# A tuned two-layer expert network on one core: the tasks that choose experts and build gates are cut in two, and one norm's rows go to another PSUM bank

## The chip, the core and the metric

The kernel runs on one core of a Trainium2 chip. The core has a matrix engine (PE, with its weight loads shown apart as PEld), a vector engine (DVE), a scalar engine (ACT), a general engine (POOL) and a queue that issues DMAs (SP). Each engine takes its instructions in the order in which the program lists them, and the engines wait for one another through semaphores. SBUF is the working memory; PSUM holds the results of matmuls in eight banks of 512 f32 per partition. The metric is the device time of one execution in microseconds (us); lower is better.

## What is computed

256 tokens of width 1024 pass through two layers and then a third block with two gated feed-forwards (`ffn1`, `ffn2`) around a token mixer. In each of the two layers a mixer is followed by this expert step (`peer`):

```python
q = (t @ w_q).reshape(n_tok, 8, 2, 128)
sc = jnp.einsum('thpd,hpnd->thpn', q, sub_keys)
s1, i1 = lax.top_k(sc[:, :, 0], 16)
s2, i2 = lax.top_k(sc[:, :, 1], 16)
cand = (s1[..., :, None] + s2[..., None, :]).reshape(n_tok, 8, 256)
top_s, pos = lax.top_k(cand, 16)
eidx = jnp.take_along_axis(cidx, pos, axis=-1)
gate = jax.nn.softmax(top_s, axis=-1)
hid = jax.nn.gelu(jnp.einsum('td,thkd->thk', tc, u[ec]), approximate=False)
out = jnp.einsum('thk,thkd->td', gc * hid, v[ec])
```

So each token has, for each of 8 heads, two lists of 128 scores; the 16 best of each list give 256 sums, and the 16 best sums name 16 of 16384 experts. The kernel multiplies all 16384 rows of `u` and `v` and lets the gates be zero for those not chosen. Everything is f32; each f32 product is made of three matmuls over a high and a low part.

## The kernel before

**Weights.** Every matrix comes from HBM as a sequence of 128x1024 f32 tiles, about 800 in all. For each tile SP issues a DMA into `wraw` (3 buffers), ACT rounds it to the high part `whi` (L178), DVE subtracts to get the low part `wlo` (L179), both with 3 buffers, and PE uses the pair in 24 matmuls (L350 to L352: `hi` by `hi`, `hi` by `lo`, `lo` by `hi`, eight times). The first instruction that needs `wlo` is the third of the 24, on L352. `W.get()` for tile k first issues the rounding and the split of tile k+2. So the split of a tile is issued up to two tiles ahead of its use and can't run further ahead, since its buffers are those of the tile that PE has just left. The next DMA into a `wraw` buffer waits until both ACT and DVE have read it.

**Side work.** Between weight tiles other work is put into the engines' streams by a small list of tasks (`Tasks`). Each task has a cost, a number written into the code; `bg.tick(budget)` is called once for each weight tile, adds its budget to a credit, and runs tasks from the front of the list as long as the credit is above zero. The cost only decides at which tile a task's instructions stand; how long they take is another matter. While `u` is multiplied the budget is 1.35 for a tile (`TK_U`), later the mean that empties the list (`bg.spread`).

**The choice of experts.** `peer` is called twice (layer 0 and layer 1). For each of two tiles of 128 tokens (`tt`) and four pairs of heads (`g`), `chosen(tt, g)` queues a group of tasks: two `keys16` (each the 16 best of two lists of 128), `make_cand` (the sums), `cand16` (the 16 best of two lists of 256), `gate_a`, `gate_b`, `gate_c` (softmax of the best, and the experts' numbers by one-hot products), and for `tt` 0 the writing of numbers and a scatter by POOL. That is eight groups a layer, spread over the 16 tiles of `w_q` and about the first 70 of the 128 tiles of `u`. The scores come from PE and ACT, the softmax's `exp` is ACT's; the rest of a group is DVE's. The 16 best are found by `top16`, five instructions for a list: the best 8 (MAX8), their places (FIND_INDEX8), the list without them (MATCH_REPLACE8), again the best 8 and their places; where places or values are looked up a short MATCH_VALUE_LOAD runs first. `top16` gets two lists at a time and alternates between them, step by step.

**The gates.** `gates(half, ...)` builds the dense gates of 8 tokens a step for token tile 1: `make` (DVE, and POOL for the second half), `mult` (16 short matmuls), `fold` (DVE multiplies the result from PSUM into the hidden values). One task runs `mult` of the step before, `make`, and `fold` of two steps before. Half 0 lies in the second part of `u`, half 1 in the first half of `v`.

**PSUM.** Two pools share the eight banks: `mm` (4, for the main products) and `acc` (4, for the sums of `v` and for side work). In `ffn1` the norm object `TwoNorms` makes two sets of per-token factors. `n.bcast()` spreads the first over all partitions (short matmuls into a bank, copied out by ACT on L452) and `n.settle()`, called from `after()`, spreads the second in the same way and queues the scaling of `h`. Both take the bank from `n.newps`, here `mmtile`.

Of the kernel before, what the change touches and what calls it, by code (L numbers as in the profile page):

```python
# [277 lines left out]
def _program(tc, nc, glob, wpool, mmp, accp, drp, ins, out, scat, stop):  # L278
# [16 lines left out]
    h = glob.tile([128, 8, TALL], F32, name="h")  # L295
# [16 lines left out]
    bg = Tasks()  # L312
# [23 lines left out]
    gcol, at = {}, 0  # L336
# [470 lines left out]
    def peer(l, n, close_parts, open_parts):  # L807
# [11 lines left out]
        gt0 = sp.tile([128, 128], F32, name="gt0")  # L819
# [10 lines left out]
        at = [(64 - NA) * 256]  # L830
# [8 lines left out]
        sc = [carve(2048).rearrange("p (q n) -> p q n", q=16) for _ in range(2)]  # L839
        cand = [carve(512) for _ in range(2)]  # L840
        zb = [carve(256) for _ in range(2)]
# [36 lines left out]
                V.max_index(out=idx[:, 8:16], in_max=val[:, 8:16], in_values=z)  # L878

        def keys16(tt, q):  # L880
            top16([(m16[tt][:, q + i], ix[tt][:, q + i], sc[tt][:, q + i], zb[i][:, 0:128]) for i in range(2)])

        def make_cand(tt, g):
            m = m16[tt].rearrange("p (h two) k -> p h two k", two=2)
# [1 line left out]
                            m[:, 2 * g:2 * g + 2, 0, :, None].to_broadcast([128, 2, 16, 16]),  # L886
                            m[:, 2 * g:2 * g + 2, 1, None, :].to_broadcast([128, 2, 16, 16]), op=ALU.add)

        def cand16(tt, g):
            top16([(t16[tt][:, 2 * g + i], pos[tt][:, g * 32 + i * 16:g * 32 + i * 16 + 16], cand[tt][:, i * 256:i * 256 + 256],  # L890
                    zb[i]) for i in range(2)])

        def gate_a(tt, g):
            w = (gt1 if tt else gt0)[:, 32 * g:32 * g + 32].rearrange("p (h k) -> p h k", h=2)
# [7 lines left out]
            V.tensor_copy(abf[tt], ab[tt].rearrange("p h s k -> p (h s k)"))  # L902

        def gate_b(tt, g):
            w = (gt1 if tt else gt0)[:, 32 * g:32 * g + 32].rearrange("p (h k) -> p h k", h=2)
            V.tensor_tensor(oh[tt], abf[tt][:, :, None].to_broadcast([128, 64, 16]),
                            io[:, None, 0:16].to_broadcast([128, 64, 16]), op=ALU.is_equal)
            V.tensor_reduce(gs[tt], w, op=ALU.add, axis=AX.X)
            o4 = oh[tt].rearrange("p (q k) a -> p q k a", q=4)
            V.tensor_tensor(o4, o4, ixf[tt][:, :, None, :].to_broadcast([128, 4, 16, 16]), op=ALU.mult)  # L910
            V.reciprocal(gs[tt], gs[tt])
# [40 lines left out]

        def chosen(tt, g):
            at = bg.add_apart(lambda: scores(g, tt))
            for i in range(2):
                bg.add(2.05, lambda q=g * 4 + 2 * i: keys16(tt, q), at)
            bg.add(0.6, lambda: make_cand(tt, g))
            bg.add(3.4, lambda: cand16(tt, g))
            bg.add(0.6, lambda: gate_a(tt, g))
            bg.add(2.4, lambda: gate_b(tt, g))  # L960
            bg.add(1.2, lambda: gate_c(tt, g))
            if tt == 0:
                bg.add(0.3, lambda: place(g))
                bg.add(0.0, lambda: (scatter(2 * g), scatter(2 * g + 1)))
# [38 lines left out]
        def gates(half, newps, cost):  # L1003
            st = {}

            E = nc.gpsimd if half else V

            def make(q):
                s = slice(q * 8, q * 8 + 8)
                js = slice(half * 64, half * 64 + 64)  # L1010
                a = sp.tile([128, 8, 128], F16, name="ga", bufs=2)
                b = sp.tile([128, 8, 64], F16, name="gb", bufs=1)
                bh = sp.tile([128, 8, 64], F16, name="gbh", bufs=2)
                bl = sp.tile([128, 8, 64], F16, name="gbl", bufs=2)
                V.tensor_tensor(b, n8[:, None, js].to_broadcast([128, 8, 64]), e2T[:, s, None].to_broadcast([128, 8, 64]), op=ALU.is_equal)
                V.tensor_tensor(a, n8[:, None, :].to_broadcast([128, 8, 128]), e1T[:, s, None].to_broadcast([128, 8, 128]), op=ALU.is_equal)
                E.tensor_tensor(bh, b, gh[:, s, None].to_broadcast([128, 8, 64]), op=ALU.mult)
                E.tensor_tensor(bl, b, gl[:, s, None].to_broadcast([128, 8, 64]), op=ALU.mult)
                st[q] = (a, bh, bl)

            def mult(q):
                a, bh, bl = st.pop(q)
                ps = newps()
                for t in range(8):
                    T_.matmul(ps[:, t * 64:t * 64 + 64], a[:, t], bh[:, t], start=True, stop=False)  # L1025
                    T_.matmul(ps[:, t * 64:t * 64 + 64], a[:, t], bl[:, t], start=False, stop=True)
                P.broken = False
                st[("p", q)] = ps

            def fold(q):  # L1030
                pv = st.pop(("p", q)).rearrange("p (t j) -> p j t", t=8)
                t = slice(128 + q * 8, 128 + q * 8 + 8)
                for j0, j1 in ((0, NA), (NA, 64)) if half == 0 else ((64, 128),):
                    hv = Ha[:, j0:j1, t] if j1 <= NA else Hb[:, j0 - NA:j1 - NA, t]
                    V.scalar_tensor_tensor(hv, pv[:, j0 - half * 64:j1 - half * 64], 1.0 / GSCALE, hv, op0=ALU.mult, op1=ALU.mult)

            def step(q):
                if 0 <= q - 1 < 16:
                    mult(q - 1)
                if q < 16:  # L1040
                    make(q)
                if 0 <= q - 2 < 16:
                    fold(q - 2)

            for q in range(18):
                bg.add(cost, lambda q=q: step(q))


        xn = Plain(xh, xl)
# [589 lines left out]
    nxt.win = [0, 128, 256]  # L1639

    def after():
        n.settle()
        unflip(sp, hk, flip, BT)
    ffn(0, n, nxt, after=after)
# [37 lines left out]
```

## Time and profile before

| | |
|---|---|
| median of 3 runs | 2381.51 us (2380.91 to 2381.56) |
| the profiled execution | 2374.57 us, of which its span is 2372.8 us |
| PE busy | 2353.3 us, 99% of the span |
| DVE busy | 1839.7 us, 78% |
| ACT busy | 1206.4 us, 51% |
| POOL busy | 646.7 us, 27% |
| chain that ended last | PE 89%, DVE 7%, ACT 2% |
| granted PE clock | 0.999 of full speed over the span |

PE's busy time is that of pipelined matmuls whose ends are modelled, so 99% says only that PE nearly always has something in flight. What a stage costs is read from where PE starts late, and from what it waits for there.

### The profile page before, as it was taken

How to read it: one execution, taken by the hardware profiler on the slowest of the kernel's cores; microseconds unless marked ns; L12 is line 12 of the kernel's file. 1: busy time of each engine (PE TensorE's matmuls, PEld its weight loads, DVE VectorE, ACT ScalarE, POOL GpSimd, SP SyncE). 2: the span in 40 equal slices, each digit the busy share in tenths (PEclk: the TensorE clock that was granted, in tenths of full speed). 3: DMA queues.
4: the chain of work that ended last, by engine and by line, in shares of the span. 5: the costliest groups of instructions: out<-in, count | busy, mean ns of one | idle time of the engine just before them, and what ended most of it. 6: DMA issues, size and time to landing. Idle time of an engine off the chain costs nothing.

```text
span 2372.8 us, 50631 instructions
## 1 busy us (share of the span) xinstructions
PE 2353.3 (99%) x20556; PEld 2292.3 (97%) x20556; DVE 1839.7 (78%) x3513; ACT 1206.4 (51%) x1750; POOL 646.7 (27%) x433
## 2 busy tenths in 40 slices
PE   9999999999999999999999999999999999999999
PEld 7799999999999999999999999999999998789999
DVE  6788997887996668788987879986677655768774
ACT  4555555444445555556554444455555443446543
POOL 2006878732330000018778603310010000200000
PEclk9999999999999999999999999999999999999999
DMA  7577887765666665557777756666655555335555
GB/s 246 182 259 205 234 236 197 187 191 196 205 209 217 220 215 190 204 174 181 188 197 184 187 183 210 207 211 221 223 195 185 177 178 178 118 101 183 194 188 171
DMA packets 170938, 464.39 MB, mean 196 GB/s; under 512 B 52400, under 2 KB 54456, under 8 KB 170320
## 3 DMA queue, kind: packets, MB, share of 16 engines
q1 hardware_dynamic: 117584, 419.06, 52.8%
q0 software_dynamic: 43760, 25.25, 8.0%
q10 hardware_dynamic: 9360, 16.84, 1.9%
q8 instruction: 161, 2.64, 0.5%
q14 instruction: 73, 0.60, 0.1%
HBM read 443.09 MB, written 17.99 MB: 194 GB/s over the span
## 4 chain that ended last, share of the span: by engine, by line
PE 89%; DVE 7%; ACT 2%; DMA 1%; issue 1%; SPq 0%; POOL 0%; ACTq 0%; DVEq 0%; POOLq 0%
PE mm L350 18%; PE mm L351 17%; PE mm L352 17%; PE acc L350 10%; PE acc L351 10%; PE acc L352 10%; PE mm L287 3%; PE acc L287 3%; DVE wlo L179 3%; DMA wraw<-in_u 1%; ACT whi L178 1%; PE acc L291 0%; DVE Hb L874 0%; DVE Hb L872 0%; PE mm L1025 0%
## 5 line engine op out<-in xcount | busy, mean ns | idle before, releaser
L179 DVE TENSOR_TENSOR wlo<-wraw,whi 128x1024 fp32r<-128x1024 f32 (+2 forms) x798 | 995.3, 1251 | 397.4 <-ACT whi L178 386.4
L178 ACT CAST whi<-wraw 128x1024 fp32r<-128x1024 f32 (+2 forms) x798 | 833.4, 1046 | 627.5 <-PE mm L351 192.0
L350 PE MATMUL mm<-xh,whi 128*128 128x256 f32 (+1 forms) x2632 | 735.1, 279 | 0.0
L352 PE MATMUL mm<-xh,wlo 128*128 128x256 f32 (+1 forms) x2632 | 729.5, 277 | 3.6 <-DVE wlo L179 3.5
L351 PE MATMUL mm<-xl,whi 128*128 128x256 f32 (+1 forms) x2632 | 728.5, 277 | 0.0
L350 PE MATMUL acc<-xh,whi 128*128 128x256 f32 x2048 | 568.6, 278 | 0.5 <-ACT xh L364 0.5
L351 PE MATMUL acc<-xl,whi 128*128 128x256 f32 x2048 | 565.8, 276 | 0.2
L352 PE MATMUL acc<-xh,wlo 128*128 128x256 f32 x2048 | 565.5, 276 | 0.0
L936 POOL DMA_INDIRECT gates<-gt,idx x256 | 477.3, 1865 | 233.1 <-issue 71.6
L350 PEld LDWEIGHTS mm<-xh,whi 128*128 128x128 f32 x2632 | 494.3, 188 | 7.3 <-issue 6.4
L352 PEld LDWEIGHTS mm<-xh,wlo 128*128 128x128 f32 x2632 | 494.4, 188 | 5.6 <-DVE wlo L179 5.5
L351 PEld LDWEIGHTS mm<-xl,whi 128*128 128x128 f32 x2632 | 494.9, 188 | 0.0
L350 PEld LDWEIGHTS acc<-xh,whi 128*128 128x128 f32 x2048 | 384.5, 188 | 0.9 <-ACT xh L364 0.9
L351 PEld LDWEIGHTS acc<-xl,whi 128*128 128x128 f32 x2048 | 384.6, 188 | 0.5 <-DVE xl L365 0.5
L352 PEld LDWEIGHTS acc<-xh,wlo 128*128 128x128 f32 x2048 | 384.6, 188 | 0.0
L350 PE MATMUL mm<-ph,whi 128*128 128x256 f32 (+1 forms) x800 | 225.9, 282 | 0.0
L351 PE MATMUL mm<-pl,whi 128*128 128x256 f32 (+1 forms) x800 | 224.7, 281 | 0.0
L352 PE MATMUL mm<-ph,wlo 128*128 128x256 f32 (+1 forms) x800 | 224.7, 281 | 0.0
L351 PEld LDWEIGHTS mm<-pl,whi 128*128 128x128 f32 x800 | 150.5, 188 | 0.2
L350 PEld LDWEIGHTS mm<-ph,whi 128*128 128x128 f32 x800 | 150.4, 188 | 0.1
L352 PEld LDWEIGHTS mm<-ph,wlo 128*128 128x128 f32 x800 | 150.5, 188 | 0.0
L1097 ACT ACTIVATE Hb<-mm 128x512 f32<-128x512 f32 x112 | 67.2, 600 | 161.1 <-PE mm L352 157.2
(344 smaller groups left out, 3038.3 us busy)
## 6 DMA issues: line engine op xcount, KB each, us to landing
wraw<-in_u SPq DMA_DIRECT2D x256, 512.0 KB
wraw<-in_v SPq DMA_DIRECT2D x256, 512.0 KB
wraw<-in_ffn_in SPq DMA_DIRECT2D x88, 512.0 KB
wraw<-in_mix_in SPq DMA_DIRECT2D x51, 512.0 KB
gates<-zt ACTq DMA_DIRECT2D x64, 256.0 KB
wraw<-in_wq SPq DMA_DIRECT2D x32, 512.0 KB
gj<-gates POOLq DMA_DIRECT2D x64, 256.0 KB
wraw<-in_ffn_out SPq DMA_DIRECT2D x32, 512.0 KB
```

Of the source, the lines that this page charges most:

```text
L178: self.nc.scalar.copy(hi[:, :cols], raw[:, :cols])
L179: self.nc.vector.tensor_tensor(lo[:, :cols], raw[:, :cols], hi[:, :cols].bitcast(F32), op=ALU.subtract)
L287: return T_.matmul(*a, **k)
L350: T_.matmul(ps, wh, mh, start=start, stop=False, **kw)
L351: T_.matmul(ps, wh, ml, start=False, stop=False, **kw)
L352: T_.matmul(ps, wl, mh, start=False, stop=stop, **kw)
L936: b = nc.gpsimd.indirect_dma_start(out=flat, out_offset=bass.IndirectOffsetOnAxis(ap=idx[:, i:i + 1], axis=0), in_=gt0[:, i:i + 1], in_off ...
L1097: A.activation(Haf[:, j * 256:j * 256 + 512] if j < NA else Hbf[:, (j - NA) * 256:(j - NA) * 256 + 512], ps, AF.Gelu)
```

## The change

`top16` is called with one list at a time: each `keys16` task of two lists becomes two tasks of one, with half the cost each, and `cand16` becomes two tasks of 1.7. `gate_b` is cut after its first product (`gate_b`, `gate_m`), and the `fold` of the gates becomes a task of its own behind the step. In `ffn1`, `after()` sets `n.newps` to `acctile` ahead of `n.settle()`. No arithmetic is added or left out.

```diff
--- before.py
+++ after.py
@@ -878,7 +878,7 @@
                 V.max_index(out=idx[:, 8:16], in_max=val[:, 8:16], in_values=z)
 
         def keys16(tt, q):
-            top16([(m16[tt][:, q + i], ix[tt][:, q + i], sc[tt][:, q + i], zb[i][:, 0:128]) for i in range(2)])
+            top16([(m16[tt][:, q], ix[tt][:, q], sc[tt][:, q], zb[q % 2][:, 0:128])])
 
         def make_cand(tt, g):
             m = m16[tt].rearrange("p (h two) k -> p h two k", two=2)
@@ -886,9 +886,9 @@
                             m[:, 2 * g:2 * g + 2, 0, :, None].to_broadcast([128, 2, 16, 16]),
                             m[:, 2 * g:2 * g + 2, 1, None, :].to_broadcast([128, 2, 16, 16]), op=ALU.add)
 
-        def cand16(tt, g):
+        def cand16(tt, g, i):
             top16([(t16[tt][:, 2 * g + i], pos[tt][:, g * 32 + i * 16:g * 32 + i * 16 + 16], cand[tt][:, i * 256:i * 256 + 256],
-                    zb[i]) for i in range(2)])
+                    zb[i])])
 
         def gate_a(tt, g):
             w = (gt1 if tt else gt0)[:, 32 * g:32 * g + 32].rearrange("p (h k) -> p h k", h=2)
@@ -902,9 +902,11 @@
             V.tensor_copy(abf[tt], ab[tt].rearrange("p h s k -> p (h s k)"))
 
         def gate_b(tt, g):
-            w = (gt1 if tt else gt0)[:, 32 * g:32 * g + 32].rearrange("p (h k) -> p h k", h=2)
             V.tensor_tensor(oh[tt], abf[tt][:, :, None].to_broadcast([128, 64, 16]),
                             io[:, None, 0:16].to_broadcast([128, 64, 16]), op=ALU.is_equal)
+
+        def gate_m(tt, g):
+            w = (gt1 if tt else gt0)[:, 32 * g:32 * g + 32].rearrange("p (h k) -> p h k", h=2)
             V.tensor_reduce(gs[tt], w, op=ALU.add, axis=AX.X)
             o4 = oh[tt].rearrange("p (q k) a -> p q k a", q=4)
             V.tensor_tensor(o4, o4, ixf[tt][:, :, None, :].to_broadcast([128, 4, 16, 16]), op=ALU.mult)
@@ -952,12 +954,14 @@
 
         def chosen(tt, g):
             at = bg.add_apart(lambda: scores(g, tt))
+            for i in range(4):
+                bg.add(1.03, lambda q=g * 4 + i: keys16(tt, q), at)
+            bg.add(0.6, lambda: make_cand(tt, g))
             for i in range(2):
-                bg.add(2.05, lambda q=g * 4 + 2 * i: keys16(tt, q), at)
-            bg.add(0.6, lambda: make_cand(tt, g))
-            bg.add(3.4, lambda: cand16(tt, g))
+                bg.add(1.7, lambda i=i: cand16(tt, g, i))
             bg.add(0.6, lambda: gate_a(tt, g))
-            bg.add(2.4, lambda: gate_b(tt, g))
+            bg.add(1.2, lambda: gate_b(tt, g))
+            bg.add(1.2, lambda: gate_m(tt, g))
             bg.add(1.2, lambda: gate_c(tt, g))
             if tt == 0:
                 bg.add(0.3, lambda: place(g))
@@ -1039,11 +1043,11 @@
                     mult(q - 1)
                 if q < 16:
                     make(q)
-                if 0 <= q - 2 < 16:
-                    fold(q - 2)
 
             for q in range(18):
-                bg.add(cost, lambda q=q: step(q))
+                bg.add(0.7 * cost, lambda q=q: step(q))
+                if q > 1:
+                    bg.add(0.3 * cost, lambda q=q: fold(q - 2))
 
 
         xn = Plain(xh, xl)
@@ -1639,6 +1643,7 @@
     nxt.win = [0, 128, 256]
 
     def after():
+        n.newps = acctile
         n.settle()
         unflip(sp, hk, flip, BT)
     ffn(0, n, nxt, after=after)
```

What this does to the streams is shown at three places. In these rows `waits` names the engines or queues whose semaphores an instruction waits for (DVE_49 in a DVE row is DVE waiting for its own earlier instruction), and `Hb` stands for all small buffers of the choice, which are carved out of one tile.

The first place is DVE in layer 0, at the first pair of heads of token tile 1, from one split of a weight tile (`wlo`) to the next ones. Before, `make_cand` (L885) and the whole of `cand16` stand between two splits, with two lists in turn:

```order
L179 TENSOR_TENSOR wlo<-wraw,whi 128x1024 [waits DMAHW4_49,PE_49,Activation_49]
L885 TENSOR_TENSOR Hb<-Hb 128x512
L870 MAX Hb<-Hb 128x8 [waits DVE_49]
L870 MAX Hb<-Hb 128x8
L872 MAX_INDEX Hb<-Hb 128x8 [waits DVE_49] x2
L874 MATCH_REPLACE Hb<-Hb 128x256 x2
L876 MAX Hb<-Hb 128x8 [waits DVE_49] x2
L878 MAX_INDEX Hb<-Hb 128x8 [waits DVE_49] x2
L179 TENSOR_TENSOR wlo<-wraw,whi 128x1024 [waits DMAHW6_49,PE_49,Activation_49]
```

After, one list stands there and the other behind the next two splits; each list's five instructions follow each other, and three of the five wait for the one right ahead of them:

```order
L179 TENSOR_TENSOR wlo<-wraw,whi 128x1024 [waits DMAHW4_49,PE_49,Activation_49]
L885 TENSOR_TENSOR Hb<-Hb 128x512
L870 MAX Hb<-Hb 128x8 [waits DVE_49]
L872 MAX_INDEX Hb<-Hb 128x8 [waits DVE_49]
L874 MATCH_REPLACE Hb<-Hb 128x256
L876 MAX Hb<-Hb 128x8 [waits DVE_49]
L878 MAX_INDEX Hb<-Hb 128x8 [waits DVE_49]
L179 TENSOR_TENSOR wlo<-wraw,whi 128x1024 [waits DMAHW6_49,PE_49,Activation_49]
L179 TENSOR_TENSOR wlo<-wraw,whi 128x1024 [waits DMAHW7_49,PE_49,Activation_49]
L870 MAX Hb<-Hb 128x8
L872 MAX_INDEX Hb<-Hb 128x8 [waits DVE_49]
L874 MATCH_REPLACE Hb<-Hb 128x256
```

The `keys16` tasks change in the same way: of the two lists, 128 long, the second follows the first or stands a tile later.

The second place is DVE at the `gate_a` and `gate_b` of the same group. Before, both stand between the same two splits (L896 to L902, then L906 to L911):

```order
L179 TENSOR_TENSOR wlo<-wraw,whi 128x1024 [waits DMAHW0_49,PE_49,Activation_49]
L896 TENSOR_TENSOR Hb<-Hb 128x32
L898 CAST Hb<-Hb 128x64
L900 TENSOR_SCALAR Hb<-Hb 128x2x16 [waits DVE_49]
L901 TENSOR_SCALAR Hb<-Hb 128x2x16
L902 CAST Hb<-Hb 128x64 [waits DVE_49]
L906 TENSOR_TENSOR Hb<-Hb 128x1024 [waits DVE_49]
L908 TENSOR_REDUCE Hb<-Hb 128x2 [waits Activation_49]
L910 TENSOR_TENSOR Hb<-Hb 128x1024 [waits DVE_49]
L911 RECIPROCAL Hb<-Hb 128x2 [waits DVE_49]
L179 TENSOR_TENSOR wlo<-wraw,whi 128x1024 [waits DMAHW2_49,PE_49,Activation_49]
```

After, a split of a weight tile stands behind the first product (L905), and the rest of the old `gate_b` (L910 to L913) follows it:

```order
L179 TENSOR_TENSOR wlo<-wraw,whi 128x1024 [waits DMAHW1_49,PE_49,Activation_49]
L896 TENSOR_TENSOR Hb<-Hb 128x32
L898 CAST Hb<-Hb 128x64
L900 TENSOR_SCALAR Hb<-Hb 128x2x16 [waits DVE_49]
L901 TENSOR_SCALAR Hb<-Hb 128x2x16
L902 CAST Hb<-Hb 128x64 [waits DVE_49]
L905 TENSOR_TENSOR Hb<-Hb 128x1024 [waits DVE_49]
L179 TENSOR_TENSOR wlo<-wraw,whi 128x1024 [waits DMAHW2_49,PE_49,Activation_49]
L910 TENSOR_REDUCE Hb<-Hb 128x2
L912 TENSOR_TENSOR Hb<-Hb 128x1024 [waits DVE_49]
L913 RECIPROCAL Hb<-Hb 128x2 [waits DVE_49]
L179 TENSOR_TENSOR wlo<-wraw,whi 128x1024 [waits DMAHW3_49,PE_49,Activation_49]
```

The third place is PE in `ffn1`, at the spreading of the two sets of factors (L287) and the first matmuls of the next weight tile. Before:

```order
L287 MATMUL mm<-ident,nry 128x16 [waits DVE_49,PE_49]
L287 MATMUL mm<-ident,nry 128x128 [waits DVE_49]
L287 MATMUL mm<-ident,nry 128x128
L287 MATMUL mm<-ident,nry 128x128 [waits Activation_49]
L287 MATMUL mm<-ident,nry 128x128
L350 MATMUL mm<-ph,whi 128x272 [waits DVE_49]
L351 MATMUL mm<-pl,whi 128x272
```

After, the second set goes to an `acc` bank and waits for nothing, and the wait for ACT stands at the first matmul of the next tile, whose bank is now the one that the first set used:

```order
L287 MATMUL mm<-ident,nry 128x16 [waits DVE_49,PE_49]
L287 MATMUL mm<-ident,nry 128x128 [waits DVE_49]
L287 MATMUL mm<-ident,nry 128x128
L287 MATMUL acc<-ident,nry 128x128 x2
L350 MATMUL mm<-ph,whi 128x272 [waits Activation_49]
L351 MATMUL mm<-pl,whi 128x272
```

## Rows read from the trace of the kernel before

**Rows 1.** The page: span, then busy time, its share and instructions of each engine.
```profile
span 2372.8 us, 50631 instructions
...
PE 2353.3 (99%) x20556; PEld 2292.3 (97%) x20556; DVE 1839.7 (78%) x3513; ACT 1206.4 (51%) x1750; POOL 646.7 (27%) x433
```

**Rows 2.** Waits of PE's weight loads, whole run, 245:346, 1117:1238.2: us, times, longest.
```profile
PEld mm L352 <- DVE wlo L179: 5.5, 10, 1.1
...
PEld mm L352 <- DVE wlo L179: 2.9, 6, 0.8
...
PEld mm L352 <- DVE wlo L179: 2.4, 3, 1.1
```

**Rows 3.** Timeline of PE at one of these waits: start, duration in us, instruction.
```profile
258.44 0.28 PE L351 MATMUL mm<-xl,whi 128*128 128x256 f32 x1
259.34 0.39 PE L352 MATMUL mm<-xh,wlo 128*128 128x256 f32 x1 [0.62 <-DVE wlo L179]
```

**Rows 4.** Windows: us, then each engine's busy us (instructions), clock, DMA share, GB/s.
```profile
1117.00:1238.20 121.20, 119.36 (x1047) 118.77 (x1046) 114.16 (x318) 69.85 (x81) 96.84 (x52) 1.00 0.75 189
248.60:373.10 124.50, 122.72 (x1053) 121.56 (x1052) 116.51 (x334) 70.61 (x81) 95.87 (x50) 1.00 0.85 233
1014.20:1117.00 102.80, 102.80 (x924) 102.53 (x924) 90.20 (x266) 59.70 (x75) 50.20 (x28) 1.00 0.63 175
148.30:248.60 100.30, 100.30 (x905) 100.19 (x904) 89.10 (x253) 58.21 (x75) 49.96 (x27) 1.00 0.80 231
```

**Rows 5.** Timeline of PE: where two runs of 44 weight tiles begin and end.
```profile
250.40 0.28 PE L352 MATMUL mm<-xh,wlo 128*128 128x256 f32 x1
...
375.60 0.28 PE L352 MATMUL mm<-xh,wlo 128*128 128x256 f32 x1
...
1118.47 0.28 PE L352 MATMUL mm<-xh,wlo 128*128 128x256 f32 x1
...
1240.93 0.28 PE L352 MATMUL mm<-xh,wlo 128*128 128x256 f32 x1
```

**Rows 6.** Timeline of DVE: the splits of the 25th tile and the next, layer 1.
```profile
1115.75 2.36 DVE L179 TENSOR_TENSOR wlo<-wraw,whi 128x1024 fp32r<-128x1024 f32 x2
```

**Rows 7.** Timeline of DVE: begin and end of a keys16 task, of a cand16 task.
```profile
272.39 0.48 DVE L870 MAX8 Hb<-Hb 128x8 f32<-128x128 f32 x2
...
274.74 1.21 DVE L179 TENSOR_TENSOR wlo<-wraw,whi 128x1024 fp32r<-128x1024 f32 x1
...
281.19 0.76 DVE L870 MAX8 Hb<-Hb 128x8 f32<-128x256 f32 x2
...
284.88 1.21 DVE L179 TENSOR_TENSOR wlo<-wraw,whi 128x1024 fp32r<-128x1024 f32 x1
```

**Rows 8.** Timeline of DVE inside one gate_a.
```profile
260.54 0.17 DVE L900 TENSOR_SCALAR Hb<-Hb 128x32 uint32<-128x32 uint32 x1
260.63 0.17 DVE L901 TENSOR_SCALAR Hb<-Hb 128x32 uint32<-128x32 uint32 x1
260.83 0.20 DVE L902 CAST Hb<-Hb 128x64 f32<-128x64 uint32 x1
```

**Rows 9.** Timeline of ACT, then of DVE, behind a gate_a in layer 1.
```profile
1124.91 0.23 ACT L897 ACTIVATE gt<-gt 128x32 f32<-128x32 f32 x1 [1.51 <-DVE gt L896]
...
1126.95 1.99 ACT L178 CAST whi<-wraw 128x1024 fp32r<-128x1024 f32 x2
...
1128.03 1.23 DVE L179 TENSOR_TENSOR wlo<-wraw,whi 128x1024 fp32r<-128x1024 f32 x1 [2.62 <-ACT whi L178]
```

**Rows 10.** Timeline of ACT, then of PE, at the second norm's rows in ffn1.
```profile
1784.09 0.39 ACT L452 COPY nbc<-mm 128x272 f32<-128x272 f32 x1 [3.65 <-PE mm L287]
...
1784.53 0.71 PE L287 MATMUL mm<-ident,nry 128*128 128x128 f32 x4 [0.47 <-ACT nbc L452]
1785.01 0.39 PE L350 MATMUL mm<-ph,whi 128*128 128x272 f32 x1
```

**Rows 11.** Windows of one line, L352: us, PE busy (instructions), PEld busy, clock, DMA.
```profile
348.00:380.00 32.00, 25.45 (x91) 17.01 (x91) 1.00 0.86 231
```

## The prediction

> **What bounds the kernel now.** I read the page first: the span is 2372.8 us and PE has something in flight for 99% of it [rows 1]. So the change can only gain where PE starts late, and it loses wherever it makes PE start later. Next I read who PE waits for. In the whole run its weight loads for L352, the first use of `wlo`, wait for DVE's split 10 times, 5.5 us together; 6 of these, 2.9 us, lie in the choice of layer 0 and 3, 2.4 us, in that of layer 1 [rows 2]. At one of them PE goes from 258.44 to 259.34 between two matmuls [rows 3]. So all that shorter tasks can win there is about 5.3 us and what follows from it.
>
> Then I asked why the split is late. Two stretches of 44 weight tiles hold all nine waits. Counted in DVE's order they run from the split of the 25th tile of `u` (excluded) to that of the 69th, at 248.6 to 373.1 in layer 0 (A) and at 1117 to 1238.2 in layer 1 (B). DVE is busy for 116.5 of 124.5 us in A and for 114.2 of 121.2 in B [rows 4]. PE takes 375.60 - 250.40 = 125.2 us for the same tiles in A and 122.5 in B [rows 5]; without its 2.4 us of waiting a tile in B costs 120.1 / 44 = 2.73. DVE has only 8.0 and 7.0 us to spare, and it can't be far ahead: in B the split of the 25th tile, the first of a pair of 2.36 us that begins at 1115.75, ends at about 1117.0 and is used at 1118.47, 1.5 us later [rows 5, 6]. PE is bound by the weights here, but DVE is a close second.
>
> **The change, part by part.**
>
> *The lists taken one at a time.* No instruction is added. A `keys16` of two lists takes 274.74 - 272.39 = 2.35 us, 1.175 a list; a `cand16` takes 284.88 - 281.19 = 3.69, 1.845 a list [rows 7]. These times belong to two lists in turn, where a result is read one instruction later. The trace has no list by itself, so I take the nearest rows for what it costs to read a result at once. In `gate_a`, L901 doesn't need L900 and starts 0.09 us after it, before L900's 0.17 us are over. L902 reads what L901 wrote and starts 0.20 us after it, 0.03 after its end [rows 8]. So such a step costs 0.11 to 0.12 us more. In a single list three of five steps are of this kind: places behind best, best behind list without them, places behind best. That is 3 x 0.115 = 0.35 us a list: 1.52 and 2.19. Below, the bound is 0; above, I see no reason for more.
>
> In each stretch the order has 16 lists of 128 and 10 of 256 before, 17 and 10 after. Before: 16 x 1.175 + 10 x 1.845 = 37.2 us. After: 17 x 1.52 + 10 x 2.19 = 47.7. DVE's work grows by 10.5 us, to 127.0 in A and 124.7 in B. Both are more than PE now needs for these tiles, 125.2 and 122.5. Behind each instruction that waits stand the rest of its list and the next split; PE waits for that split on L352, and SP's DMA into the `wraw` buffer that the split frees.
>
> The Trainium skill says otherwise: in "VectorE: DVE Perf Modes", section "The DRAIN you can't avoid", a vector instruction never starts before the pipe is empty, so that a semaphore behind each of a chain costs nothing extra. By that rule the 10.5 us would be 0. The trace doesn't agree, since L901 starts 0.08 us before L900's end [rows 8].
>
> *What DVE's spare time takes up.* Of the 8.0 and 7.0 us, what is lost only because DVE was early goes away when it is late. What stays is the wait behind `gate_a`: its `exp` on ACT starts at 1124.91, ACT then has a Gelu of its own to do, `whi` starts at 1126.95, and the split begins at 1128.03 after 2.62 us of idle DVE [rows 9]. In the order after, one such place remains in each stretch (`gate_a` alone between two splits, ahead of the Gelu). At one other place the cut of `gate_b` takes about 1.3 us of cover away, since L905 alone stands where two products of this kind (each about as long as the split's 1.23 us, [rows 9], and partly under each other) stood; I take half of that. So 2.6 + 0.7 = 3.3 us stay. A: 127.0 + 3.3 - 125.2 = +5.1. B: 124.7 + 3.3 - 122.5 = +5.5. PE's nine old waits are inside these numbers, as 125.2 and 122.5 contain them.
>
> Bounds: if nothing stays idle and the 1.5 us of lead are spent too, A gives +0.3 and B +0.7. If all idle time of now stays, A gives +9.8 and B +9.2.
>
> *The tiles ahead of the stretches.* There DVE has 100.3 - 89.1 = 11.2 and 102.8 - 90.2 = 12.6 us to spare [rows 4]; the lists add 6.0 by the same count (16 lists of 128 and 6 of 256 before, 15 and 6 after: 29.9 us against 35.9). I book 0, and 2 at most.
>
> *`fold` as a task of its own; lower cost sums.* The cost sum of the gates falls from 18 to 18 x 0.7 + 16 x 0.3 = 17.4, so its pace falls by 3% and the list still empties ahead of the drain. Nine of ten waits for `wlo` are in the choice [rows 2], so the gates have no wait to win. A `fold` one tile later holds its PSUM bank longer, but four banks serve three results in flight. 0. Were that cover gone, a wait at each of 32 steps would cost some 0.1 us, 3 us in all.
>
> *The bank in `ffn1`.* The second set's matmuls start at 1784.53, 0.05 after ACT's copy ends at 1784.48, and the next tile's first matmul follows at 1785.01 [rows 10]. In the new order these matmuls wait for nothing, but the next tile's first now waits for the same copy. So what is won is their own time, 1785.01 - 1784.53 = 0.5 us, and not the whole wait. -0.5; bounds 0 and -0.5 - 0.47.
>
> **Sum.** +5.1 + 5.5 - 0.5 = +10.1 us. The profiled execution took 2374.6 us, so 2384.7 by it; the runs' median, 2381.5, lies 6.9 above that execution, and the prediction is for such runs: 2381.5 + 10 = 2391.5. The ends are 0.3 + 0.7 - 0.5 = +0.5 (2382) and 9.8 + 9.2 + 2 = +21 (2402.5).
>
> **The rivals.**
>
> *Shorter tasks are enough (not slower).* The longest work on lists between two splits falls from 3.7 us to 3.0 (two lists of 128) or 2.2 (one of 256). If the idle time is nearly all taken up and the lead spent, the two stretches lose 1 to 4 us: 2384. For it: most idle time of DVE today is that of an engine that is early. Against it: the sums 127.0 and 124.7 leave no room for any wait. It decides when less than about 1 us of idle stays in each stretch.
>
> *A single list costs no more (faster).* This is what the page's rule gives. Then DVE keeps its 116.5 and 114.2 us, the lumps are shorter and the nine waits go: -5.3. In 348 to 380, behind one of them, 91 L352 take 32 us, 2.81 us a tile against 2.73 in B [rows 11]; if that slower pace comes from the wait, 14 tiles give 1.2 more. With -0.5 in `ffn1`: 2374.5. For it: the lumps are what delays the split now. Against it: [rows 8]. It decides below 0.05 us a dependent step.
>
> *The slower pace comes more often.* If every new wait can set PE to 2.81 us a tile, up to 44 x 0.08 = 3.5 us a stretch could come; but where DVE sets the pace, a slower PE only fills its waits. It widens the top, no more.
>
> **How the numbers follow.** Slower as forecast 0.68; about the same, by the first rival, 0.21; faster, by the second, 0.11. A measurement here tells about 0.2%, 4.8 us, from no change: 2376.7 to 2386.3 counts as the same. The range 2379 to 2400 leaves out the faster case and the last of the top.
>
> **What would show it.** Right: a list of 128 takes about 1.5 us from its first MAX8 to the next instruction, one of 256 about 2.2; DVE's busy time grows by 96 x 0.35 = 34 us; its idle time in A and B falls by more than half; PE's waits for `wlo` come to some 15 us in place of 5.5, many short ones where there were few; the wait for `nbc` in `ffn1` stands at L350. Wrong: lists of 1.2 and 1.85 us (then the second rival), or lists of 1.5 with few waits (then DVE's idle time gave more room than I allow).

## The result and the profile after

The changed kernel takes 2404.35 us (median of 5 runs, 2402.57 to 2406.59); the kernel before, timed beside it, 2381.51 (5 runs, 2378.65 to 2384.03). The ratio is 1.0097, 95% interval 1.0085 to 1.0108: slower by 23 us (20 to 26). The forecast was 2391.5, 10 us slower, with a range of 2379 to 2400. The sign was right, the size less than half of what was measured, and the time lies outside the range.

The page of the changed kernel, its span and busy times (us, share, instructions), answers to [rows 1]:

```profile
span 2402.9 us, 50637 instructions
...
PE 2367.1 (99%) x20556; PEld 2299.5 (96%) x20556; DVE 1871.1 (78%) x3513; ACT 1206.9 (50%) x1750; POOL 686.8 (29%) x433
```

DVE has 31.4 us more to do and, a surprise, POOL 40.1. Next, who PE waits for: its weight loads' waits in the whole run, in the 44 tiles of A and in those of B (us, times, longest), which answer to [rows 2], and then PE's own waits for POOL in the whole run:

```profile
PEld mm L352 <- DVE wlo L179: 22.9, 35, 1.3
...
PEld mm L352 <- DVE wlo L179: 9.2, 13, 1.3
...
PEld mm L352 <- DVE wlo L179: 9.0, 14, 1.3
...
PE mm L1029 <- POOL gbh L1021: 2.0, 2, 1.0
PE mm L1030 <- POOL gbl L1022: 1.6, 2, 0.8
```

The first three are the wait that was forecast, larger; the last two are new and were not forecast. The windows of B and A, for the same tiles as in [rows 4] (us, then busy us of PE, PEld, DVE, ACT and POOL, clock, DMA share, GB/s), and PE's timeline at their ends, as in [rows 5]:

```profile
1135.20:1265.70 130.50, 123.83 (x1053) 120.90 (x1052) 122.44 (x328) 71.01 (x81) 100.94 (x54) 1.00 0.72 178
252.90:384.30 131.40, 124.25 (x1052) 121.46 (x1051) 123.31 (x332) 71.39 (x81) 105.22 (x55) 1.00 0.84 218
```

```profile
252.94 0.38 PE L352 MATMUL mm<-xh,wlo 128*128 128x256 f32 x1
...
385.12 0.28 PE L352 MATMUL mm<-xh,wlo 128*128 128x256 f32 x1
...
1135.43 0.28 PE L352 MATMUL mm<-xh,wlo 128*128 128x256 f32 x1
...
1266.51 0.28 PE L352 MATMUL mm<-xh,wlo 128*128 128x256 f32 x1
```

PE takes 385.12 - 252.94 = 132.2 us for A and 131.1 for B, where it took 125.2 and 122.5 [rows 5]. Reading PE's timeline at the same tile all along the program gives the whole difference of the two profiled executions (30.1 us, where the medians lie 23 apart: the profiled execution of the kernel before was a quick one):

| part of the program, by PE's first L352 of a tile | layer 0 | layer 1 |
|---|---|---|
| `w_q` and what is ahead of it | +0.2 | +0.9 |
| first tiles of `u`, up to A or B | +2.4 | +2.4 |
| the 44 tiles of A, B | +7.0 | +8.6 |
| rest of `u` (half 0 of the gates) | +0.5 | 0.0 |
| first 62 tiles of `v` (half 1 of the gates) | +3.6 | +2.7 |
| `ffn1` / all behind it (unchanged code) | | -0.5 / +2.3 |

**A list by itself.** DVE's timeline of a `keys16` of one list in the changed kernel, from its first MAX8 to the next split:

```profile
255.50 0.29 DVE L870 MAX8 Hb<-Hb 128x8 f32<-128x128 f32 x1
255.82 0.09 DVE L872 MATCH_VALUE_LOAD Hb<-Hb 128x8 f32 x1
255.90 0.29 DVE L872 FIND_INDEX8 Hb<-Hb 128x8 uint32<-128x128 f32 x1
...
257.08 1.21 DVE L179 TENSOR_TENSOR wlo<-wraw,whi 128x1024 fp32r<-128x1024 f32 x1
```

It takes 1.58 us, against 1.175 in a pair [rows 7]: the MATCH_VALUE_LOAD that needs MAX8's result starts 0.03 us behind its end, as L902 did in [rows 8]. A list of 256, from its first MAX8 to the next split, takes 173.87 - 171.62 = 2.25:

```profile
171.62 0.42 DVE L870 MAX8 Hb<-Hb 128x8 f32<-128x256 f32 x1
...
173.87 1.21 DVE L179 TENSOR_TENSOR wlo<-wraw,whi 128x1024 fp32r<-128x1024 f32 x1
```

The forecast had 1.52 and 2.19.

**DVE's idle time that stays.** ACT's and then DVE's timeline behind the `gate_a` that stands alone in B, the place forecast from [rows 9]:

```profile
1226.95 0.23 ACT L897 ACTIVATE Hb<-Hb 128x32 f32<-128x32 f32 x1 [2.87 <-DVE Hb L896]
1227.20 1.28 ACT L1101 ACT_TABLE_LOAD   x1
1228.50 0.60 ACT L1101 ACTIVATE Hb<-mm 128x512 f32<-128x512 f32 x1
1228.99 1.98 ACT L178 CAST whi<-wraw 128x1024 fp32r<-128x1024 f32 x2
...
1230.06 1.23 DVE L179 TENSOR_TENSOR wlo<-wraw,whi 128x1024 fp32r<-128x1024 f32 x1 [2.63 <-ACT whi L178]
```

ACT has been ready for 2.87 us when L896 gives it the `exp`; then it loads the Gelu's table, 1.28 us, does the Gelu, and only then comes the rounding that the split needs. There are four such places in B, 2.63, 1.05, 0.73 and 0.49 us, 4.9 together, and four in A, 4.8 together; 3.3 were forecast for each.

**`ffn1`.** PE's, then ACT's timeline at the second norm's rows, as in [rows 10]:

```profile
1812.18 0.61 PE L287 MATMUL acc<-ident,nry 128*128 128x128 f32 x4
1812.82 0.40 PE L350 MATMUL mm<-ph,whi 128*128 128x272 f32 x1
...
1812.38 0.39 ACT L452 COPY nbc<-mm 128x272 f32<-128x272 f32 x1 [3.64 <-PE mm L287]
```

The four matmuls run beside ACT's copy, and L350 starts 0.05 us behind its end: the wait has moved there, and 0.5 us is won, as forecast.

**The gates' second half.** POOL's timeline at the first two steps of half 1 in layer 0, after:

```profile
565.94 1.86 POOL L1021 TENSOR_TENSOR gbh<-gb,gh 128x512 f16<-128x512 f16 x1 [73.42 <-DVE gb L1019]
...
572.69 5.23 POOL L1021 TENSOR_TENSOR gbh<-gb,gh 128x512 f16<-128x512 f16 x1 [3.33 <-DVE gb L1019]
577.89 1.03 POOL L1022 TENSOR_TENSOR gbl<-gb,gl 128x512 f16<-128x512 f16 x1
```

The second step begins 572.69 - 565.94 = 6.75 us behind the first; its `gbh` is done at 577.92 and its `gbl` at 578.92, and PE, which comes for both one step later, stands for 1.0 and 0.8 us. Before, the same rows of POOL were these:

```profile
555.93 1.86 POOL L1017 TENSOR_TENSOR gbh<-gb,gh 128x512 f16<-128x512 f16 x1 [55.62 <-DVE gb L1015]
...
564.35 3.77 POOL L1017 TENSOR_TENSOR gbh<-gb,gh 128x512 f16<-128x512 f16 x1 [5.00 <-PE mm L1026]
568.08 1.03 POOL L1018 TENSOR_TENSOR gbl<-gb,gl 128x512 f16<-128x512 f16 x1
```

The steps lay 8.4 us apart and PE found everything ready.

### The profile page after: what moved, and what is told of

It is laid out like the page before. It is cut to its first block, busy times and chain, and to the rows that moved or that the text cites. A ratio compares the mean times of both kernels' runs of the same rounds, so it can differ in the third digit from the quotient of the medians.

```text
span 2402.9 us, 50637 instructions
## 1 busy us (share of the span) xinstructions
PE 2367.1 (99%) x20556; PEld 2299.5 (96%) x20556; DVE 1871.1 (78%) x3513; ACT 1206.9 (50%) x1750; POOL 686.8 (29%) x433
## 4 chain that ended last, share of the span: by engine, by line
PE 83%; DVE 12%; ACT 2%; issue 2%; POOL 1%; DMA 0%; SPq 0%; ACTq 0%; POOLq 0%
PE mm L350 16%; PE mm L352 16%; PE mm L351 15%; PE acc L350 9%; PE acc L351 9%; PE acc L352 9%; DVE wlo L179 5%; PE mm L287 4%; PE acc L287 3%; DVE Hb L872 1%; DVE Hb L878 1%; DVE Hb L876 1%; DVE Hb L874 1%; ACT whi L178 1%; DVE Hb L870 1%
## 5 line engine op out<-in xcount | busy, mean ns | idle before, releaser
L352 PE MATMUL mm<-xh,wlo 128*128 128x256 f32 (+1 forms) x2632 | 733.0, 279 | 16.0 <-DVE wlo L179 15.6
L350 PE MATMUL mm<-xh,whi 128*128 128x256 f32 (+1 forms) x2632 | 736.2, 280 | 1.0 <-ACT whi L178 1.0
L350 PE MATMUL acc<-xh,whi 128*128 128x256 f32 x2048 | 569.8, 278 | 0.5 <-ACT xh L364 0.5
L352 PE MATMUL acc<-xh,wlo 128*128 128x256 f32 x2048 | 566.7, 277 | 0.0
L352 PEld LDWEIGHTS mm<-xh,wlo 128*128 128x128 f32 x2632 | 494.4, 188 | 23.0 <-DVE wlo L179 22.9
L350 PEld LDWEIGHTS mm<-xh,whi 128*128 128x128 f32 x2632 | 494.3, 188 | 8.7 <-issue 6.4
L350 PEld LDWEIGHTS acc<-xh,whi 128*128 128x128 f32 x2048 | 385.3, 188 | 0.9 <-ACT xh L364 0.9
L352 PEld LDWEIGHTS acc<-xh,wlo 128*128 128x128 f32 x2048 | 385.3, 188 | 0.0
L350 PE MATMUL mm<-ph,whi 128*128 128x256 f32 (+1 forms) x800 | 226.1, 283 | 0.0
L352 PE MATMUL mm<-ph,wlo 128*128 128x256 f32 (+1 forms) x800 | 224.9, 281 | 0.0
L1021 POOL TENSOR_TENSOR gbh<-gb,gh 128x512 f16<-128x512 f16 x32 | 91.2, 2849 | 281.2 <-DVE gb L1019 281.2
L350 PEld LDWEIGHTS mm<-ph,whi 128*128 128x128 f32 x800 | 150.5, 188 | 0.3 <-ACT nbc L452 0.2
L352 PEld LDWEIGHTS mm<-ph,wlo 128*128 128x128 f32 x800 | 150.4, 188 | 0.0
```

Of the source, the lines that this page charges most:

```text
L350: T_.matmul(ps, wh, mh, start=start, stop=False, **kw)
L352: T_.matmul(ps, wl, mh, start=False, stop=stop, **kw)
```

## The experiments

Each is told against the kernel before, timed on the same chip; gains and losses are ratio times 2380 us, with the 95% interval.

**The kernel before once more.** 

> The kernel before, once more, for a second profile of it. The first profiled execution took 2374.6 us, 6.9 less than the median of its runs. If that execution was only a quick one, this one takes 2378 to 2385 us, and its u tiles of the choice (from the split of the first to that of the 69th) take 2 to 3 us longer a layer than the 194.5 and 190.2 us of the first; if the difference lies elsewhere, these stretches agree to 1 us and another part of the program is longer.

It took 2375.1 us, span 2373.3. Neither of the two expectations came true: it was as quick as the first execution, and A and B differ from the first profile by 2 us, in opposite directions (123.2 and 124.3 us of PE, where the first had 125.2 and 122.5). So one trace tells the length of such a stretch to about 2 us; the sum of A and B is 247.5 here and 247.7 there. The median of the unprofiled runs beside it was 2380.25 (2374.2 to 2386.1). So both profiled executions of the kernel before were quick ones. What the unprofiled runs spend more isn't in a trace; a likely part, not shown, is the stretch behind `ffn1`, where the code is the same in all thirteen profiles and the last L352 of `ffn1` starts 395.0 to 401.9 us ahead of the end.

**Only the lists taken apart.**

```diff
-            top16([(m16[tt][:, q + i], ix[tt][:, q + i], sc[tt][:, q + i], zb[i][:, 0:128]) for i in range(2)])
+            top16([(m16[tt][:, q], ix[tt][:, q], sc[tt][:, q], zb[q % 2][:, 0:128])])
...
-            for i in range(2):
-                bg.add(2.05, lambda q=g * 4 + 2 * i: keys16(tt, q), at)
+            for i in range(4):
+                bg.add(1.03, lambda q=g * 4 + i: keys16(tt, q), at)
...
-            bg.add(3.4, lambda: cand16(tt, g))
+            for i in range(2):
+                bg.add(1.7, lambda i=i: cand16(tt, g, i))
```

> The kernel before with only keys16 and cand16 taken one list at a time. Theory 1 (DVE sets the pace in all of the first 68 tiles of u, and a list by itself costs it 0.35 us more): nearly the whole loss is here, 18 to 24 us over the kernel before, 2400 to 2405 us, and PE waits for wlo about 20 us. Rival A (the loss comes from the cuts of gate_b and fold and from the places that they give to the other tasks): at most 8 us over the kernel before. Rival B (PE's waits for POOL and the slow clock behind one of them are a good part): at most 14 us.

Measured: 2397.19 against 2380.25, ratio 1.0064 (1.0045 to 1.0084), +15 us (11 to 20). PE's waits for `wlo`:

```profile
PEld mm L352 <- DVE wlo L179: 21.0, 30, 1.8
```

That lies between theory 1 (18 to 24) and rival B (at most 14), and the interval reaches to both; rival A (at most 8) is out. The lists are about two thirds of the loss, not nearly all. In its trace A and B are 7.0 and 9.2 us longer than in the kernel before, together 16.2, as much as in the changed kernel (15.6): in these two stretches the lists alone are enough for the loss.

**The changed kernel with the lists back in pairs** (the same lines the other way round).

> The changed kernel with keys16 and cand16 back in pairs; the cuts of gate_b and fold and the bank in ffn1 stay. Theory 1: no more than 0 to 5 us over the kernel before (the waits for POOL in the gates' second half cost 2 to 6, the shorter gate_b and the bank give 0.5 to 2 back). Rival A: 12 us or more over the kernel before. Rival B: 7 to 12.

Measured: 2386.89, ratio 1.0027 (1.0015 to 1.0038), +6.4 us (3.6 to 9). That lies between theory 1 (0 to 5) and rival B (7 to 12), and the interval reaches to both; rival A (12 or more) is out. With the 15 above this makes 21.7 of the 23, so the two parts add up, and the second is no trifle.

**DVE longer, lists in pairs.** The instruction added at the end of `top16`:

```diff
                 V.max_index(out=idx[:, 8:16], in_max=val[:, 8:16], in_values=z)
+            V.tensor_reduce(more, skf[:, 0:608], op=ALU.add, axis=AX.X)
```

> The kernel before, lists in pairs as they are, with one more DVE instruction behind each pair that nobody needs: a sum over 608 numbers of the sub-keys per partition, about 0.70 us, twice the 0.35 us that a list by itself costs more. Nothing else is changed. Theory 1: it is DVE's time alone that counts, so this costs what the single lists cost, 15 to 24 us. Rival C (single lists lose through their order, their waits or their finer steps, not through DVE's time): under 8 us.

Measured: 2396.93, ratio 1.0069 (1.0051 to 1.0087), +16.4 us (12 to 21). Waits, then busy times:

```profile
PEld mm L352 <- DVE wlo L179: 24.7, 25, 2.7
...
PE 2364.3 (99%) x20556; PEld 2299.4 (96%) x20556; DVE 1873.2 (78%) x3561; ACT 1208.7 (50%) x1750; POOL 678.3 (28%) x433
```

33.5 us more of DVE in 48 pieces, without a wait of DVE for itself and without a cut, cost as much as the single lists do. Rival C (under 8 us) is out: it is DVE's time. The pieces also make each task 0.7 us longer, so this run by itself doesn't tell time from the length of a task; the pairs cut by step, below, do.

**Only the fold apart.**

```diff
-                if 0 <= q - 2 < 16:
-                    fold(q - 2)
...
-                bg.add(cost, lambda q=q: step(q))
+                bg.add(0.7 * cost, lambda q=q: step(q))
+                if q > 1:
+                    bg.add(0.3 * cost, lambda q=q: fold(q - 2))
```

> The kernel before with only the fold of the gates as a task of its own (0.7 and 0.3 of the old cost). Theory 1 (the gates' second half is hurt: its first two steps, which have no fold, now follow one another after 0.7 of a step instead of 1, and PE reaches the next mult before POOL has made gbh and gbl): waits of PE for POOL at L1026 and L1027 or their like, some 2 us a layer, half of the time with a fall of the granted clock behind them, 3 to 7 us over the kernel before in all. Rival D (what the paired version loses sits in the cut of gate_b): no loss, within 2 us of the kernel before, and no wait for POOL.

Measured: 2388.96 against 2383.67, ratio 1.0026 (1.0013 to 1.0038), +6 us (3 to 9). In its trace PE waits for POOL once in each layer's `v`:

```profile
PE mm L1026 <- POOL gbl L1018: 1.8, 1, 1.8
```

These two waits are 3.6 us, so rival D is out. The rest is within the interval; some of it can be the clock, which the last section shows, but behind these two waits it didn't fall.

**The fold apart, the first two steps at the whole cost.**

```diff
-                bg.add(0.7 * cost, lambda q=q: step(q))
+                bg.add(0.7 * cost if q > 1 else cost, lambda q=q: step(q))
```

> The fold as a task of its own, as before, but the first two steps of the gates, which have no fold, keep the whole cost, so that every step stands as far from the next as in the kernel before. Theory 1 (the loss of the fold on its own is PE's wait for POOL at the second step, which comes 6.8 us behind the first in place of 8.4, and what the clock does behind it): no wait for POOL, within 2 us of the kernel before. Rival G (the loss is POOL's longer gbh, 3.8 us in place of 1.9 in half of the steps, wherever they stand): POOL's gbh still 2.5 us or more on average, and 3 us or more over the kernel before.

Measured: 2379.72 against 2379.23, ratio 0.9999 (0.999 to 1.0008). No wait of PE for POOL is left in either layer's `v`, while POOL is as slow as in the changed kernel (32 `gbh`, 2829 ns each on average):

```profile
L1017 POOL TENSOR_TENSOR gbh<-gb,gh 128x512 f16<-128x512 f16 x32 | 90.5, 2829 | 268.4 <-DVE gb L1015 268.4
```

So the longer `gbh` by itself costs nothing (rival G is out). Its second step in layer 1 shows what the distance does:

```profile
1426.41 3.76 POOL L1017 TENSOR_TENSOR gbh<-gb,gh 128x512 f16<-128x512 f16 x1 [5.01 <-DVE gb L1015]
1430.14 2.01 POOL L1018 TENSOR_TENSOR gbl<-gb,gl 128x512 f16<-128x512 f16 x1
```

POOL's two products take 1432.15 - 1426.41 = 5.74 us, exactly what they take at the second step of the version with the fold apart. There the step begins 6.75 us behind the first and PE waits 1.8 us; here it begins 8.4 us behind it and PE doesn't wait.

**Only `gate_b` cut.**

```diff
-            bg.add(2.4, lambda: gate_b(tt, g))
+            bg.add(1.2, lambda: gate_b(tt, g))
+            bg.add(1.2, lambda: gate_m(tt, g))
```

> The kernel before with only gate_b cut behind its first product. Theory 1 (a split comes earlier by one product, but the cover of ACT's exp is shorter): 0 to 3 us over the kernel before, since the paired version loses 6.4 and the fold alone 5.3 of it. Rival A: 4 us or more over it.

Measured: 2383.29 against 2379.23, ratio 1.0012 (1.0003 to 1.0022), +2.9 us (0.7 to 5.2). DVE's timeline in layer 0:

```profile
206.84 1.22 DVE L905 TENSOR_TENSOR Hb<-Hb 128x1024 f32<-128x1024 f32 x1
212.68 1.23 DVE L179 TENSOR_TENSOR wlo<-wraw,whi 128x1024 fp32r<-128x1024 f32 x1 [4.62 <-ACT whi L178]
```

A split now stands behind the first product, and ACT's `exp` with its table loads stands ahead of its rounding: 4.62 us without work. Before, the second product and two small instructions lay inside this time and left 1.79 and 1.45 of it idle. The 2.9 us are within theory 1 (0 to 3), but the interval reaches into rival A (4 or more). The idle time shown isn't where PE loses: from the first tile of `u` to A, where it lies, PE takes only 0.3 us more in this trace than in the first profile of the kernel before.

**Pairs cut by step.** The third way to make tasks short: both lists' first three instructions in one task, the last two in the next (`next8` is the second half of `top16`; `cand16` is cut in the same way, at 2.05 and 1.35).

```diff
-                bg.add(2.05, lambda q=g * 4 + 2 * i: keys16(tt, q), at)
+                bg.add(1.25, lambda q=g * 4 + 2 * i: keys16(tt, q, top16), at)
+                bg.add(0.8, lambda q=g * 4 + 2 * i: keys16(tt, q, next8))
```

> The kernel before with the two-list tasks cut in another way: both lists' first three instructions (best, places, list without them) in one task, both lists' last two in the next, so that the tasks are as short as those of single lists and each result is still read one instruction later. Theory 1 (DVE's time decides, the length of a task hardly): DVE's busy time stays at 1840 us, the time is within 4 us of the kernel before. Rival E (shorter tasks by themselves help, by what PE waits for wlo now): 5 us or more faster. Rival A (short tasks hurt by where they stand): 5 us or more slower.

Measured: 2377.8 against 2383.67, ratio 0.9979 (0.9969 to 0.9989), 5 us faster (2.6 to 7.4). PE's waits for `wlo` in its trace, in place of 5.5 us in 10 [rows 2]:

```profile
PEld mm L352 <- DVE wlo L179: 2.6, 4, 1.0
```

DVE's busy time stays as it was (1838.0 us). The 5 us are rival E's number (5 or more), and the interval reaches into theory 1's (within 4): DVE's time isn't all that counts, and short tasks help too, provided that they don't make DVE longer.

**The `exp` later.**

```diff
-            A.activation(w, w, AF.Exp)
+            late = [lambda: A.activation(w, w, AF.Exp)]
+            exps.append(late)
+            W.later(lambda: late and late.pop()())
```

(`gate_c` issues it if that hasn't happened yet, and has the sum and the reciprocal.) 

> The kernel before with gate_a's exp on ACT issued behind the next weight tile's rounding instead of ahead of it, and its sum and reciprocal moved from gate_b to gate_c, which comes a tile later. It takes away the one idle time of DVE that stays in the choice when DVE sets the pace. Theory 1: DVE's idle time in the u tiles 0 to 68 falls by 2 to 4 us a layer, and as DVE is nearly the bound there, 2 to 7 us faster than the kernel before. Rival F (that idle time is only DVE being early): within 2 us.

Measured: 2382.55 against 2383.67, ratio 0.9991 (0.9981 to 1.0001): 2 us faster or nothing. By itself this is not settled. The fall of DVE's idle time by 2 to 4 us a layer isn't in its trace: in the `u` tiles of the choice it is 2.7 and 2.5 us longer than before.

**Both together, and the bank.** 

> The last two together, and the bank of ffn1 as changed: shorter tasks without longer lists, the exp later, the second norm's rows in an acc bank; the gates as before. Theory 1: the sum of the two and 0.5 more, 3 to 10 us faster than the kernel before. If shorter tasks and DVE's idle time don't matter: within 2 us.

Measured: 2373.98 against 2383.67, ratio 0.9957 (0.9941 to 0.9973), 10 us faster (6 to 14): this version beats both kernels. Its six runs (2368.7 to 2375.6) all lie below the twelve of the pairs cut by step (2375.7 to 2380.5), so on top of those the later `exp` does help: the medians lie 3.8 us apart, and the bank gives only 0.5. The windows of its B and A:

```profile
1112.80:1231.70 118.90, 118.90 (x1052) 118.90 (x1051) 114.94 (x325) 69.82 (x82) 91.46 (x47) 1.00 0.77 193
251.10:371.50 120.40, 120.22 (x1057) 119.71 (x1056) 116.68 (x334) 71.69 (x82) 93.72 (x50) 1.00 0.90 241
```

PE is busy for all of B and for 120.2 of the 120.4 us of A; there is no waiting left to win there.

**The change, mended**: pairs cut by step, the gates' first two steps at the whole cost, the rest as changed. 

> The change with its two costs taken out: two lists in a task as before, but cut by step; the gates' first two steps at the whole cost; the cut of gate_b, the fold as a task and the bank in ffn1 as changed. Theory 1: DVE's busy time back at 1840 us, no wait for POOL, 2 to 7 us faster than the kernel before. If tasks of this length at these places hurt by themselves: 3 us or more slower than it.

Measured: 2376.91 against 2379.23, ratio 0.999 (0.9981 to 1.0), 2.4 us faster or nothing (-5 of the cut by step, +2.9 of `gate_b`'s cut and -0.5 of the bank make -2.6). No wait of PE for POOL is left, and DVE is busy for 1844.2 us.

## Why the prediction was wrong

The mechanism that was forecast, DVE's time for single lists, is the larger part of the loss. But two steps of the prediction that were booked at nothing failed, the fold (6 us measured) and the tiles ahead of A and B (4.8 us), and a third term, the idle time that stays in A and B, was booked at 6.6 us and measured at 9.7.

The parts as measured are +15 for the lists, +6 for the fold, +2.9 for `gate_b`'s cut and -0.5 for the bank (read from the trace, not run by itself): 23 to 24, against 23 in the whole. The forecast had +9.2, 0, +1.4 and -0.5. Point by point:

- *The price of a single list*: right. 1.58 and 2.25 us against 1.52 and 2.19; DVE's busy time grew by 31.4 us against 34 (the gaps inside a list count as idle). The second rival, a single list that costs no more, fell with it: here it costs 0.4 us more. The prediction took that rival from the page "VectorE: DVE Perf Modes" of the Trainium skill, section "The DRAIN you can't avoid", where a semaphore behind each of eight copies cost nothing extra; these chains of small instructions don't agree. The same section also says that a next instruction that isn't held starts earlier, which the prediction's "never" leaves out; so the early start of L901 in [rows 8] doesn't contradict it.
- *The stretches A and B*: right mechanism, too small. +7.0 and +8.6 of PE's time in the changed kernel, 15.6 together, against +5.1 and +5.5, 10.6. The term that was mis-sized is the idle time that stays: 3.3 us a stretch were booked, one `gate_a` and half a product; 4.8 and 4.9 were left, at four places each. That is 3.1 of the 5.0 us missing. Another 1.4 is that PE's stretch is 0.6 to 0.8 us longer than DVE's window, and 0.5 is DVE's work with its gaps, 126.6 and 125.6 us (127.0 and 124.7 forecast). The sign "idle time in A and B falls by more than half" failed: it is 8.1 us in each stretch, 3.3 and 3.2 of it short gaps, nearly all inside the lists. One slip is in the count: the rows of A begin with the split of the 24th tile, where 18 lists of 128 stand before and after, so the lists add 28 x 0.345 = 9.7 us there and not 10.5.
- *"The tiles ahead of the stretches": 0, and 2 at most.* This step failed. In `u`'s part of them 2.4 us were lost in each layer, 4.8 in all (4.0 against the control's trace). The 11.2 and 12.6 us of DVE's spare time [rows 4] were the sum of a window of 34 tiles that had been taken for cover, without asking in which tiles it lay and what it waited for. The same tiles in the changed kernel, layer 0 and then layer 1:

```profile
148.60:252.90 104.30, 102.94 (x919) 102.19 (x917) 94.15 (x253) 59.05 (x75) 51.43 (x29) 1.00 0.80 227
1028.00:1135.20 107.20, 105.41 (x936) 104.33 (x936) 94.85 (x258) 59.88 (x75) 53.59 (x29) 1.00 0.61 168
```

DVE's work grew, but 104.30 - 94.15 = 10.2 and 12.4 us of idle time are still there. Some 2.1 us of it are gaps inside the lists; 7.8 and 8.4 us end with ACT's rounding of a tile, where it was 8.5 and 9.1 before. So some 3 us of the spare time were filled in layer 0 and some 2 in layer 1; the rest, most of it a wait for ACT, was no cover.

- *"`fold` as a task of its own; lower cost sums": 0.* This step failed, and it is the dearest one booked at nothing: +6 us. The cover that it named, four PSUM banks for three results, held. The cover that it didn't name was POOL's: the lower price moved the second step from 8.4 to 6.75 us behind the first, and POOL's products, which take up to 6.3 us there, came late for PE. The "3 us in all" that were priced for the case of that cover gone belonged to another wait, and were left out of the sum's upper end.
- *The cut of `gate_b`*: half a product, 0.7 us a stretch, was booked, 1.4 in all. Alone it costs 2.9 us (0.7 to 5.2), so the 1.4 aren't excluded. Where it costs is open: in its own trace A and B are 5.3 us longer together, but in that of the changed kernel with the lists in pairs, which has the same cut, they are not longer.
- *`ffn1`*: right, -0.5 us, and the wait stands where it was forecast.
- *PE's waits for `wlo`*: "some 15 us in place of 5.5", 22.9 measured, 18.2 of it in A and B.
- *The first rival, shorter tasks*: its mechanism is there (the pairs cut by step gain 5 us), but in this change it lies under the 34 us of DVE.
- *The third rival, the slower pace*: not needed. Most of PE's matmuls start 113 or 114 ns behind the one ahead, some 117 to 119. In A 454 of 1056 starts are of the slower kind in the kernel before, 146 in the control, which is the same kernel, and 294 after; in B 5, 148 and 132. So this differs as much between two executions of one kernel as between the kernels.

What stays open: which part of the fold's 6 us is clock, where `gate_b`'s cut costs its 2.9, and why executions of the same program differ by 12 us and more.

## What to carry to other kernels

Here, cutting a task to make it short was worth something only where the cut left each result its distance to the next reader; two chains in turn hide that distance, and the place to cut is between steps of both, not between the chains. Spare time of an engine covers work only in the same tiles, so count it tile by tile with what it waits for. Where a cost number is lowered, ask for each engine that works between two tasks (here POOL) whether it still has the time.

## What was not expected of the hardware

**POOL and DVE hold each other up, and the fold let POOL in.** POOL's `gbh` and then DVE's timeline at the third step of half 1 in the kernel before:

```profile
573.18 1.88 POOL L1017 TENSOR_TENSOR gbh<-gb,gh 128x512 f16<-128x512 f16 x1 [3.54 <-DVE gb L1015]
...
572.95 1.22 DVE L1016 TENSOR_TENSOR ga<-n,e1T 128x1024 f16<-128x1024 f16 x1
574.08 0.68 DVE L1035 SCALAR_TENSOR_TENSOR Hb<-mm,Hb 128x512 f32<-128x512 f32 x1
574.68 0.53 DVE L1068 TENSOR_TENSOR Ha<-Ha,gj 128x128 f32<-128x128 f32 x1
575.14 2.06 DVE L179 TENSOR_TENSOR wlo<-wraw,whi 128x1024 fp32r<-128x1024 f32 x1
```

and after, beside the `gbh` of 5.23 us from 572.69 that is shown above:

```profile
572.47 1.21 DVE L1020 TENSOR_TENSOR ga<-n,e1T 128x1024 f16<-128x1024 f16 x1
573.60 0.28 DVE L1072 TENSOR_TENSOR Ha<-Ha,gj 128x128 f32<-128x128 f32 x1
573.80 1.21 DVE L179 TENSOR_TENSOR wlo<-wraw,whi 128x1024 fp32r<-128x1024 f32 x1
...
576.61 0.41 DVE L365 TENSOR_TENSOR xl<-Ha,xh 128x256 fp32r<-128x256 f32 x1
```

Before, the fold (L1035, which reads PSUM) follows `ga`; POOL's product ends 0.9 us behind the end of `ga`, at 575.06, and DVE's next instructions are stretched (0.53 us in place of 0.28, 2.06 in place of 1.2). After, DVE goes on without a gap through instructions with two inputs from SBUF, none is stretched, and POOL's product ends 0.9 us behind the last of them, at 577.92. The Trainium skill, "SBUF — State Buffer", section "SBUF: two separate sides", says that the two engines share a pair of ports as an exclusive lock, which a DVE operation with two SBUF inputs holds against a POOL operation that reads SBUF. The rows agree: POOL's product gets through where the fold, with only one of its two inputs from SBUF, stands. The row after is the second step, which has no fold in either kernel (its `gbh` took 3.77 us before); over all steps, 14 of 32 `gbh` last more than 2.5 us in the changed kernel, and 1 of 32 before.

**A clock fall behind a short wait, some of the time.** The window right behind PE's wait for POOL in layer 0 of the changed kernel, and two behind the same place of the version with the lists in pairs:

```profile
579.60:583.00 3.40, 3.40 (x17) 3.40 (x17) 3.40 (x4) 0.41 (x1) 3.21 (x3) 0.50 0.08 31
```

```profile
569.80:573.20 3.40, 3.38 (x27) 3.38 (x27) 3.40 (x4) 0.41 (x1) 2.56 (x2) 0.51 0.28 106
1440.20:1443.60 3.40, 3.40 (x19) 3.40 (x18) 3.40 (x3) 0.41 (x1) 3.29 (x3) 0.50 0.02 10
```

The granted clock is 0.50, that is 1.2 GHz in place of 2.4, and 17 matmuls take 3.4 us where at 1.00 they take about 1.8 (29 in 3.0 us right behind it). PE had stood for 1.0 and 0.8 us just before. In layer 1 of the changed kernel the same wait, and at both places of the kernel with only the fold apart one of 1.8 us, came without a fall. In the table this part of the program costs 3.6 us in layer 0, where the clock fell, and 2.7 in layer 1, where it didn't.
